# First layer: the weighted head output is read out of PSUM by ScalarE, behind its own square, in place of VectorE

## The chip, the cores and the metric

The kernel runs on one core of one Trainium2 chip. The metric is the device time of one execution in microseconds (us), as the median of several runs of the same program. Five engines work side by side: TensorE (PE in the profile; PEld is its weight load), VectorE (DVE), ScalarE (ACT), GpSimd (POOL) and SyncE (SP), which here only issues DMAs. Each works through its own list of instructions in order and waits on semaphores for the others.

## The reference

A backbone of two layers over 512 latent tokens and 256 context tokens of width 1024. The first layer mixes tokens by differential attention with 8 heads, the second by grouped-query attention. The change is in the first layer, in what follows the attention of one head:

```python
o1 = sweep_attention(qq[..., 0, :], kk[..., 0, :], vv)
o2 = sweep_attention(qq[..., 1, :], kk[..., 1, :], vv)
o = o1 - lam.astype(o1.dtype) * o2
o = rms_norm(o, subln_g) * (1.0 - lam_init)          # over the head's 128 columns
o = o.reshape(o.shape[0], o.shape[1], BRANCH_WIDTH)
return (o * jax.nn.silu(gate)) @ w_out
```

`rms_norm` needs the sum of squares of a head's output and its product with the weight `subln_g`. Everything is computed to float32 accuracy.

## The kernel before, in words

A float32 product is made of three passes on TensorE: each operand is split into a rounded part and a rest (tiles `whi`/`wlo` for weights, `h` for activations, `vhi`/`vlo` for values, `ah`/`al` for attention weights), and hi*hi, hi*lo and lo*hi are added up in PSUM. A split is a ScalarE cast followed by a VectorE subtraction (L225 and L219 for weights, L1062 and L1063 for `ah`/`al`).

The first layer's attention runs from about 75 to 455 us of the span. Per head there are three chunks (`ch`) of two 128-token query blocks: two of latent queries and one of context queries. A chunk is worked off in three stages, which the planner `flow` mixes with projections of later heads:

- **Scores** (`s_units`, L994; L1023 for the context chunk) go into one pair of PSUM tiles, `sc`. VectorE takes the row maximum (L999, L1029), ScalarE the exponential (L1002, L1033), VectorE the reciprocal and the two scalings (L1005, L233, L1009, L1010, L1041), which leave the difference of the two softmaxes in a tile `p`.
- **Transposes** (`tstep`, L1059) put `p` into one of four PSUM banks `bk`; ScalarE and VectorE split it into `ah` and `al` (L1062, L1063).
- **Values** (`mstep`, `pv_mm`, L167): 18 matmuls for a latent chunk (6 for the context chunk) add up the head's output for 256 tokens in a bank. After the last, the bank is read twice and given back:

```python
nc.scalar.activation(ogs[h][:, sl], o, AF.Square)      # L1080: tile sq
scaled(EG0, gT[h][:, sl], o, subg)                     # L1081: tile gT
close(o)
...
def scaled(eng, dst, src, s_):
    if eng == "a":
        nc.scalar.activation(dst, src, AF.Copy, scale=s_)                                          # L231
    else:
        (nc.vector if eng == "v" else nc.gpsimd).tensor_scalar(dst, src, s_, 1.0, ALU.mult, ALU.mult)  # L233
```

`subg` is a column of 128 weights. That is 8 heads x 3 chunks = 24 squares and 24 scalings of 128x256 elements. Later `subln` (`subln_last` for the last head) sums the squares over the head with a matmul of ones (`colsum`: ScalarE cast L404, POOL subtraction L405, TensorE L406 and L407), takes the reciprocal root on ScalarE (L1091, L1093; for the last head L1106, L1108) and multiplies `gT` by it on VectorE (L1094, L1109).

The four banks `bk` are shared by all of it: projections of q, k, v and z (L155), transposes, value sums, sums of squares, the matmuls of the adaptive-norm weights (`grp_mm`, L835, from tile `araw`) and of the layer's gate (`gate0_finish`, L1131 and L1132, then VectorE L1133 and L1134). A bank's next user waits until its last readers are done.

Weights come in by SP's queue into a ring of two buffers, `raw`; a buffer is free for the next load when its cast L225 and its subtraction L219 are done. `gate0_finish` uses the same ring: it loads a bias (`in_ada_b`) into one buffer and a norm weight (`in_post_g`) into the next (L1116).

The order of instructions on each engine is not the program's text order. `flow` writes the steps down by a table of due times, and the scheduler of the Tile layer then orders each engine's instructions by priorities and by its own estimate of when each is ready. So another engine for one instruction can move instructions on all engines.

Of the kernel before, what the change touches and what calls it, by code (L numbers as in the profile page):

```python
# [68 lines left out]
GFIN = (10, 13)  # L69
QLAG = 2.87  # L70
QTR = 5.35
EG0 = 'v'
EP0 = 'v'
EN1 = 'p'
ESW = 'v'
# [12 lines left out]
def tile_backbone(  # L88
# [55 lines left out]
    def close(o):  # L144
        lru.append(held.pop(id(o))[1])
# [83 lines left out]
# [5 lines that stand above are left out]
# [582 lines left out]
    with tc.tile_pool(name="t0", bufs=1) as t0:  # L816
# [233 lines left out]
        def pv_steps(h, at, ch, after, ts, ms):  # L1050
# [15 lines left out]
            def mstep(kt):  # L1066
# [7 lines left out]
                if kt == kts[-2]:  # L1074
# [5 lines left out]
                    nc.scalar.activation(ogs[h][:, sl], o, AF.Square)  # L1080
                    scaled(EG0, gT[h][:, sl], o, subg)  # L1081
                    close(o)
# [733 lines left out]
```

## Time and profile before

| | |
|---|---|
| median of three runs | 792.33 us |
| the profiled execution's own time | 792.09 us |
| its span, first to last instruction | 790.3 us |
| mean granted TensorE clock | 0.998 |
| instructions in the span | 14199 |
| HBM read / written | 70.56 MB / 2.10 MB |

The profile's page gives busy time by engine, the chain of work that ended last, and groups of instructions by line; the trace behind it can be asked for windows of time, for one tile, or for who waited for whom. In a group's row `x24: 459/476/485` is a count and the shortest, median and longest duration in ns; in a row with bars, `| 11.4, 476 | 3.8 <-ACT sq L1080 3.6` is busy time in us, mean duration in ns, then the engine's idle time just before these instructions and what ended it. A row of a timeline begins with the start in us from the span's start and the duration. Matmuls are pipelined: neighbours overlap in such rows, so that a busy share near 100% says that TensorE had something in flight, not that it could not go faster.

### The profile page before, as it was taken

How to read it: one execution, taken by the hardware profiler on the slowest of the kernel's cores; microseconds unless marked ns; L12 is line 12 of the kernel's file. 1: busy time of each engine (PE TensorE's matmuls, PEld its weight loads, DVE VectorE, ACT ScalarE, POOL GpSimd, SP SyncE). 2: the span in 40 equal slices, each digit the busy share in tenths (PEclk: the TensorE clock that was granted, in tenths of full speed). 3: DMA queues.
4: the chain of work that ended last, by engine and by line, in shares of the span. 5: the costliest groups of instructions: out<-in, count | busy, mean ns of one | idle time of the engine just before them, and what ended most of it. 6: DMA issues, size and time to landing. Idle time of an engine off the chain costs nothing.

```text
span 790.3 us, 14199 instructions
## 1 busy us (share of the span) xinstructions
PE 776.0 (98%) x5446; PEld 699.4 (88%) x5446; DVE 544.8 (69%) x988; ACT 455.2 (58%) x994; POOL 286.4 (36%) x386
## 2 busy tenths in 40 slices
PE   8999999999999999999999999999999999999996
PEld 6688888987888898788979998899999999989986
DVE  4656787996888656776588853567458987565634
ACT  5546555665665644765468843565456676676632
POOL 1111443733236331344313311585436554234101
PEclk9999999999999999999999999999999999999999
DMA  9933211141323222233330151041423512010102
GB/s 340 383 101 144 80 54 58 51 134 41 134 80 108 94 81 67 94 107 108 117 97 28 54 209 59 1 141 54 160 82 102 148 46 81 28 54 27 54 27 107
DMA packets 35092, 77.77 MB, mean 98 GB/s; under 512 B 3408, under 2 KB 10064, under 8 KB 35024
## 3 DMA queue, kind: packets, MB, share of 16 engines
q1 hardware_dynamic: 31168, 71.05, 26.8%
q10 hardware_dynamic: 3856, 5.81, 2.1%
q8 instruction: 43, 0.70, 0.4%
q14 instruction: 25, 0.20, 0.1%
HBM read 70.56 MB, written 2.10 MB: 92 GB/s over the span
## 4 chain that ended last, share of the span: by engine, by line
PE 89%; DMA 5%; DVE 2%; ACT 2%; POOL 1%; issue 1%; SPq 0%; DVEq 0%; ACTq 0%; POOLq 0%
PE bk L155 57%; PE bk L167 9%; PE sc L155 8%; PE sc L994 5%; PE bk L1059 3%; PE bk L1558 3%; PE bk L835 1%; DMA xnt<-in_xcT 1%; DMA ag<-in_ada 1%; DMA lamb<-in_a_lam 1%; PE sc L1023 1%; DMA xnt<-in_xlT 1%; POOL wlo L219 1%; DMA raw<-in_b_w 1%; PE bk L407 0%
## 5 line engine op out<-in xcount | busy, mean ns | idle before, releaser
L155 PE MATMUL bk<-whi,h 128*128 128x256 f32 (+1 forms) x1184 | 244.0, 299 | 0.0
L155 PE MATMUL bk<-h,whi 128*128 128x512 f32 (+2 forms) x864 | 228.2, 346 | 0.0
L155 PEld LDWEIGHTS bk<-whi,h 128*128 128x128 f32 x1184 | 191.9, 191 | 10.2 <-issue 3.7
L155 PE MATMUL bk<-wlo,h 128*128 128x256 f32 (+1 forms) x592 | 175.7, 299 | 0.0
L155 PEld LDWEIGHTS bk<-h,whi 128*128 128x128 f32 x864 | 150.5, 189 | 17.0 <-issue 2.7
L155 PE MATMUL bk<-h,wlo 128*128 128x512 f32 (+2 forms) x432 | 149.3, 346 | 0.0
L155 PEld LDWEIGHTS bk<-wlo,h 128*128 128x128 f32 x592 | 112.6, 191 | 4.6 <-issue 1.5
L219 DVE TENSOR_TENSOR wlo<-raw,whi 128x1024 fp32r<-128x1024 f32 (+1 forms) x66 | 82.9, 1258 | 33.5 <-ACT whi L225 33.4
L155 PEld LDWEIGHTS bk<-h,wlo 128*128 128x128 f32 x432 | 81.5, 189 | 7.9 <-issue 1.1
L225 ACT CAST whi<-raw 128x1024 fp32r<-128x1024 f32 x64 | 67.1, 1049 | 32.3 <-PE bk L155 27.9
L999 DVE TENSOR_REDUCE sm<-sc 128x1 f32<-128x768 f32 (+1 forms) x68 | 60.6, 917 | 23.2 <-PE sc L994 23.1
L1002 ACT ACTIVATE p<-sc,sm 128x768 f32<-128x768 f32 (+1 forms) x68 | 59.7, 880 | 23.5 <-DVE sm L999 19.0
L219 POOL TENSOR_TENSOR sz<-sz,za 128x192 f32<-128x192 f32 (+1 forms) x48 | 32.7, 703 | 101.8 <-ACT za L199 101.8
L233 POOL TENSOR_SCALAR p<-p,sm 128x768 f32<-128x768 f32 x32 | 31.6, 987 | 57.3 <-DVE sm L1544 46.0
L1562 DVE TENSOR_TENSOR al<-bk,ah 128x512 fp32r<-128x512 f32 x48 | 32.1, 686 | 18.1 <-ACT ah L1561 17.9
L994 PE MATMUL sc<-qk,qk 64*128 64x384 f32 (+1 forms) x396 | 43.9, 351 | 0.7 <-ACT p L1002 0.7
L219 POOL TENSOR_TENSOR qk<-qr,qk 128x256 fp32r<-128x256 f32 x42 | 32.3, 800 | 33.0 <-ACT qk L889 33.0
L1062 ACT CAST ah<-bk 128x512 fp32r<-128x512 f32 x56 | 31.8, 589 | 20.3 <-PE bk L1059 19.5
L405 POOL TENSOR_TENSOR sqs<-sq,sqs 128x384 fp32r<-128x384 f32 (+2 forms) x16 | 19.4, 1214 | 59.2 <-ACT sqs L404 52.4
L1543 ACT ACTIVATE p<-sc,sm,qrs 128x768 f32<-128x768 f32 x32 | 31.9, 997 | 15.6 <-DVE sm L1540 9.4
L1063 DVE TENSOR_TENSOR al<-bk,ah 128x512 fp32r<-128x512 f32 x56 | 37.2, 681 | 4.4 <-ACT ah L1062 4.2
L219 POOL TENSOR_TENSOR qr<-qr,rope 128x256 f32<-128x256 f32 x28 | 26.0, 948 | 39.0 <-DMA sw<-qr 35.3
(241 smaller groups left out, 1541.1 us busy)
## 6 DMA issues: line engine op xcount, KB each, us to landing
raw<-in_a_w SPq DMA_DIRECT2D x28, 512.0 KB, 3.4
araw<-in_ada_w SPq DMA_DIRECT2D x12, 1024.0 KB, 5.2
raw<-in_b_w SPq DMA_DIRECT2D x20, 512.0 KB, 4.1
ag<-in_ada SPq DMA_DIRECT2D x16, 512.0 KB, 8.0
raw<-in_w_out SPq DMA_DIRECT2D x16, 512.0 KB, 3.5
sw<-qr ACTq DMA_DIRECT2D x32, 128.0 KB, 2.1
gw<-in_ada_w SPq DMA_DIRECT2D x8, 512.0 KB, 4.7
xnt<-in_xlT SPq DMA_DIRECT2D x4, 512.0 KB, 5.6
```

The source lines that it names most:

```text
L155: i = nc.tensor.matmul(o, a, b, start=start, stop=stop)
L167: nc.tensor.matmul(o, v[:, kt + e, c], a[:, e * 256:e * 256 + 256], start=first and i == 0, stop=last and i == 5)
L219: eng.tensor_tensor(dst[:, i:i + n], a[:, i:i + n], b[:, i:i + n], op)
L225: nc.scalar.copy(hi, r)
L233: (nc.vector if eng == "v" else nc.gpsimd).tensor_scalar(dst, src, s_, 1.0, ALU.mult, ALU.mult)
L994: prev = nc.tensor.matmul(sc[m][:, j if nk == T else m, :w], a[r, tok], b[r, c], start=i == 0, stop=i == 2)
L999: nc.vector.tensor_reduce(mx, scv, AX.XY if nk == T else AX.X, ALU.max, negate=True)
L1002: nc.scalar.activation(pv_, scv, AF.Exp, bias=mx, accum_out=l[:, m:m + 1])
L1062: nc.scalar.copy(ah, tr)
L1063: nc.vector.tensor_tensor(al, tr, f32(ah), ALU.subtract)
L1543: nc.scalar.activation(pt.rearrange("p (j n) -> p j n", j=2), scv, AF.Exp, scale=sr, bias=nmx, accum_out=l)
L1562: nc.vector.tensor_tensor(al, tr, f32(ah), ALU.subtract)
```

## The change

One constant is set from VectorE to ScalarE:

```diff
-EG0 = 'v'
+EG0 = 'a'
```

`EG0` is used in one place, L1081 (shown above). So the 24 scalings leave VectorE (`TENSOR_SCALAR`, L233) and become ScalarE `ACTIVATE` instructions with the function `Copy` and the column `subg` as their scale (L231). Nothing else in the text changes, and on each engine the same other instructions remain; but from the first of these scalings on, through the end of the first layer, the scheduler gives all engines another order.

Three places of that order. First ScalarE at the end of head 4 (tile `gT_2808`): rows that stay have no sign, those with + are new there.

```order
 L1080 ACTIVATE sq_3460<-bk_71 128x256
+L231 ACTIVATE gT_2808<-bk_71,subg 128x256
 L404 CAST sqs_3616<-sq_3460 128x384
 L225 CAST whi_3565<-raw_3563 128x1024
 L866 ACTIVATE qr_3329<-bk_70 128x256
 L1080 ACTIVATE sq_3460<-bk_68 128x256
+L231 ACTIVATE gT_2808<-bk_68,subg 128x256
 L1002 ACTIVATE p_3667,sm_3652<-sc_72,sm_3665 128x768
 L1091 ACTIVATE sq_3460<-bk_71,eps 128x384
```

Each scaling stands directly behind the square of the same bank; the exponential L1002 and the root's logarithm L1091 are behind both. The same holds at all 24 places.

Second VectorE in the middle of head 2, where the first half of the layer's gate is made (`gate_0`, `gate_1`; `raw_2159` is the bias, `raw_2161` the norm weight; `raw_2135` and `raw_2141` are the two weight loads ahead of them in the ring).

```order
+L219 TENSOR_TENSOR wlo_2138<-raw_2135,whi_2137 128x1024
 L1029 TENSOR_REDUCE sm_2197<-sc_72 128x2
 L1063 TENSOR_TENSOR al_2156<-bk_68,ah_2155 128x512
-L219 TENSOR_TENSOR wlo_2138<-raw_2135,whi_2137 128x1024
 L931 TENSOR_TENSOR vlo_1945<-bk_71,vhi_1944 128x256
+L1133 TENSOR_TENSOR gate_0_691<-bk_69,raw_2159 128x512
 L219 TENSOR_TENSOR wlo_2144<-raw_2141,whi_2143 128x1024
-L1133 TENSOR_TENSOR gate_0_691<-bk_69,raw_2159 128x512
 L1134 TENSOR_TENSOR gate_0_691<-gate_0_691,raw_2161 128x512
+L1029 TENSOR_REDUCE sm_2205<-sc_73 128x2
 L1063 TENSOR_TENSOR al_2180<-bk_68,ah_2179 128x512
 L1133 TENSOR_TENSOR gate_1_692<-bk_71,raw_2159 128x512
```

The subtraction `wlo_2138`, which frees the buffer for the bias, moves up two places, and the addition of the bias (L1133, `gate_0`) now stands ahead of `wlo_2144`, which frees the buffer for the norm weight. On ScalarE the cast `whi_2137` moves up three places with it; five of the matmuls that read the weights it replaces now stand ahead of the context scores (L1023), not behind them.

Third TensorE a little later, where it needs what VectorE makes there (`bk_68` is read by `al_2180`, `bk_71` by `gate_1`).

```order
+L155 MATMUL bk_70<-h_594,whi_1937 128x512
+L155 MATMUL bk_70<-h_593,wlo_1938 128x512
 L1059 MATMUL bk_68<-ident,p_1915 128x128
 L1059 MATMUL bk_68<-ident,p_2032 128x128
...
-L835 MATMUL bk_70<-araw_1986,s_129 32x512 x4
 L167 MATMUL bk_71<-ah_2155,vhi_1944 128x256 x2
 L167 MATMUL bk_71<-ah_2155,vlo_1945 128x256 x2
...
+L835 MATMUL bk_70<-araw_1986,s_129 32x512 x4
```

The four matmuls L835 stood between the transposes into `bk_68` and the value sum in `bk_71`; now that sum follows the transposes directly, and L835 comes after it.

## The prediction

> **What bounds the kernel now.** I read the page first: busy time by engine, then the chain of work that ended last.
>
> ```profile
> PE 776.0 (98%) x5446; PEld 699.4 (88%) x5446; DVE 544.8 (69%) x988; ACT 455.2 (58%) x994; POOL 286.4 (36%) x386
> PE 89%; DMA 5%; DVE 2%; ACT 2%; POOL 1%; issue 1%; SPq 0%; DVEq 0%; ACTq 0%; POOLq 0%
> ```
>
> TensorE is in flight 98% of the span and holds 89% of the chain; VectorE and ScalarE together hold 4%. An average hides stages, so next come windows over the stretch in which the 24 scalings run (101 to 453 us). The columns are the window, its length, then busy time and count for PE, PEld, DVE, ACT and POOL, the granted clock, the DMA share and GB/s.
>
> ```profile
> 100.00:150.00 50.00, 50.00 (x335) 43.26 (x332) 42.12 (x67) 30.15 (x63) 22.81 (x26) 1.00 0.18 58
> 150.00:200.00 50.00, 48.81 (x364) 42.33 (x363) 41.38 (x70) 30.70 (x69) 20.92 (x25) 1.00 0.27 90
> 200.00:250.00 50.00, 50.00 (x351) 44.14 (x352) 42.03 (x69) 31.40 (x64) 20.59 (x23) 1.00 0.30 102
> 250.00:300.00 50.00, 49.99 (x355) 44.53 (x355) 31.23 (x53) 25.89 (x51) 17.22 (x21) 1.00 0.29 95
> 300.00:350.00 50.00, 48.40 (x352) 42.32 (x351) 38.54 (x72) 32.67 (x73) 17.48 (x22) 1.00 0.27 91
> 350.00:400.00 50.00, 50.00 (x372) 44.84 (x371) 31.56 (x60) 24.74 (x52) 15.27 (x18) 1.00 0.32 106
> 400.00:440.00 40.00, 38.79 (x273) 34.05 (x272) 34.46 (x69) 29.75 (x68) 13.54 (x16) 1.00 0.17 53
> ```
>
> Here VectorE is the fuller of the two (31 to 42 of 50 us), ScalarE has 17 to 25 us free in each 50, and TensorE is idle for only 1.19 + 0.01 + 1.60 + 1.21 = 4.0 us in all. What other engines do reaches the end only through TensorE, so 4.0 us is about the most that relief on VectorE can return. Which waits make up these 4.0 us is in the list of who waited for whom on TensorE (us in total, times, longest):
>
> ```profile
> PE bk L835 <- DVE gT L233: 1.6, 1, 1.6
> PE bk L1059 <- DVE al L1063: 1.1, 1, 1.1
> PE sc L994 <- ACT p L1002: 0.7, 1, 0.7
> PE bk L835 <- DVE al L1063: 0.5, 1, 0.5
> ```
>
> The longest ends with one of the 24 scalings; two end with VectorE's subtraction `al`, one with ScalarE's exponential.
>
> **The change part by part.** VectorE loses 24 instructions, ScalarE gains 24 behind 24 squares that it already does. One row of the tile `gT`, one of the tile `sq` (count, shortest, median and longest ns):
>
> ```profile
> L233 DVE TENSOR_SCALAR gT<-bk,subg x24: 459/476/485, 101.2 to 453.0; 128x256 f32<-128x256 f32 x24
> L1080 ACT ACTIVATE sq<-bk x24: 375/386/423, 100.8 to 452.6; 128x256 f32<-128x256 f32 x24
> ```
>
> *Work.* VectorE gives up 24 x 0.476 = 11.4 us. The new instruction (ScalarE copy, PSUM to SBUF, scaled by a column) is not in the trace. Its neighbours are, by form, within the attention (busy us, mean ns, idle before):
>
> ```profile
> L866 ACT ACTIVATE qr<-bk 128x256 f32<-128x256 f32 x11 | 4.2, 379 | 0.0
> L1033 ACT ACTIVATE p<-sc,sm 128x256 f32<-128x256 f32 x28 | 13.0, 480 | 4.6 <-PE bk L1059 4.6
> L1091 ACT ACTIVATE sq<-bk,eps 128x384 f32<-128x384 f32 x14 | 8.1, 579 | 20.2 <-PE bk L407 20.1
> L197 ACT ACTIVATE za<-za 128x384 f32<-128x384 f32 x14 | 7.4, 527 | 0.3
> ```
>
> The same copy of this size with a constant scale takes 379 ns: the lower bound. An exponential of this size with a column as bias, which also sums, takes 480 ns: the upper bound. A logarithm with a column (579) is 52 ns over one with a constant (527), so I take the square's 386 + 52, near 0.44 us, and 24 x 0.44 = 10.6 us (9.1 to 11.5) on ScalarE. Spread over 350 us this is 1.5 us in each 50, against 17 to 25 free: hidden under TensorE. If that cover were gone, all 10.6 us would show. Likewise VectorE's 11.4 us return nothing by themselves. The sum therefore rests on places where TensorE waits.
>
> [...]
>
> *Place 1, end of head 4: the stall that the change removes.* Timeline of all engines (start, duration):
>
> ```profile
> 321.09 1.81 DVE L999 TENSOR_REDUCE sm<-sc 128x1 f32<-128x768 f32 x2
> 321.28 0.39 ACT L1080 ACTIVATE sq<-bk 128x256 f32<-128x256 f32 x1 [1.12 <-PE bk L167]
> 322.07 0.90 ACT L1002 ACTIVATE p<-sc,sm 128x768 f32<-128x768 f32 x1 [0.41 <-DVE sm L999]
> 322.82 0.47 DVE L233 TENSOR_SCALAR gT<-bk,subg 128x256 f32<-128x256 f32 x1
> 322.96 0.57 ACT L1091 ACTIVATE sq<-bk,eps 128x384 f32<-128x384 f32 x1
> 323.35 1.06 PE L835 MATMUL bk<-araw,s 128*32 128x512 f32 x8 [1.60 <-DVE gT L233]
> 324.34 0.50 PE L155 MATMUL bk<-h,whi 128*128 128x256 f32 x2
> ```
>
> The square is done at 321.67, but VectorE is inside two row maxima until 322.8, so the bank comes free at 323.3 and L835 starts at 323.35. In the changed order the copy follows the square at once: 321.67 + 0.44 = 322.1, L835 at 322.15, that is 1.2 us earlier. What is late next: behind L835 stands a projection (L155) into the bank that the logarithm L1091 reads, and L1091 stays behind the exponential L1002 (0.89 us from start to start). It would end near 322.12 + 0.89 + 0.57 = 323.58, so L155 starts at 323.6 in place of 324.34. Gain 0.7 us, not 1.6.
>
> *Place 2, the gate in head 2: a wait that the new order lengthens.*
>
> ```profile
> 184.21 0.98 PE L1023 MATMUL sc<-qk,qk 64*128 64x256 f32 x12
> 187.06 1.05 ACT L225 CAST whi<-raw 128x1024 fp32r<-128x1024 f32 x1
> 188.15 1.81 DVE L219 TENSOR_TENSOR wlo<-raw,whi 128x1024 fp32r<-128x1024 f32 x1 [0.26 <-ACT whi L225]
> 189.98 0.33 SPq L1116 DMA_DIRECT2D raw<-in_ada_b  x1
> 190.21 1.42 DVE L219 TENSOR_TENSOR wlo<-raw,whi 128x1024 fp32r<-128x1024 f32 x1
> 191.66 0.33 SPq L1116 DMA_DIRECT2D raw<-in_post_g  x1
> 193.12 0.69 DVE L1133 TENSOR_TENSOR gate<-bk,raw 128x512 f32<-128x512 f32 x1 [1.49 <-DMA raw<-in_ada_b]
> 194.77 0.69 DVE L1134 TENSOR_TENSOR gate<-gate,raw 128x512 f32<-128x512 f32 x1 [0.96 <-DMA raw<-in_post_g]
> 195.38 0.68 DVE L1063 TENSOR_TENSOR al<-bk,ah 128x512 fp32r<-128x512 f32 x1
> 195.98 0.68 DVE L1133 TENSOR_TENSOR gate<-bk,raw 128x512 f32<-128x512 f32 x1
> 196.12 0.66 PE L1059 MATMUL bk<-ident,p 128*128 128x128 f32 x4 [1.15 <-DVE al L1063]
> 196.70 1.06 PE L835 MATMUL bk<-araw,s 128*32 128x512 f32 x8
> 197.70 0.51 PE L167 MATMUL bk<-ah,vhi 128*128 128x256 f32 x2
> ```
>
> The page's group of such subtractions has a mean of 1258 ns:
>
> ```profile
> L219 DVE TENSOR_TENSOR wlo<-raw,whi 128x1024 fp32r<-128x1024 f32 (+1 forms) x66 | 82.9, 1258 | 33.5 <-ACT whi L225 33.4
> ```
>
> Each subtraction `wlo` frees a ring buffer; the load after it takes 3.1 us (189.98 to 193.12, 191.66 to 194.77). In this order the two loads overlap. In the changed order the bias's addition stands between the subtractions, so the second load starts only after the first has landed. Part of that is returned: the first cast may start when the moved matmuls are done, near 185.0, not at 187.06. Followed with these durations and 1.26 us for a `wlo`: cast done 186.05, first `wlo` 187.35, bias landed 190.5, addition and second `wlo` done 192.4, norm weight landed 195.5; then L1134 and the maximum L1029 (0.61 each from start to start) and `al`, done 197.4 against 196.06. The value sum L167 waits for the second addition, 198.05 against 197.70, with L835's 1.0 us still to do. Cost 198.05 + 1.0 - 197.70 = 1.4 us (rounded up); 0 at best, if the loads are out of the way earlier; 4.0 if the first `wlo` ends no earlier than before (189.96, and all of the rest 2.6 us later).
>
> *Everything else that is reordered*, on all engines to the end of the layer: I can name no one wait with a size, so 0, with bounds of -2.5 us (the other TensorE waits, 4.0 less Place 1's 1.6) and about +4 us (as much new waiting as there is now). Where TensorE's new order asks for a bank early, the copy helps: after a value sum the bank is free after two ScalarE instructions, 0.39 + 0.44 us, without VectorE's queue between.
>
> *Sum.* 792.09 - 0.7 + 1.4 + 0 = 792.8 us against the profiled execution (span 790.3). The median of the runs, 792.33, lies 0.24 above it, so 793.0.
>
> **Rivals.** *The copy chokes ScalarE* (slower). ScalarE works in order, and behind each copy stand exponentials and `ah` casts that TensorE's next transposes and value sums need. If TensorE had to wait for every one, it would cost 10.6 us, 803.6 with the forecast's other terms; for a third of them 3.5 us: 796.5. It decides where ScalarE has no gap between a copy and what TensorE waits for. For it: one of the four waits above ends with an exponential. Against it: 17 to 25 us free per 50. [...]
>
> *The loads at Place 2 are dearer*: 4.0 in place of 1.4, so 795.6. For it: 1.49 and 0.96 us of VectorE's idle time there already end with these loads. Against it: the moved matmuls free the weight buffer early.
>
> *The waits dissolve* (faster): the bank returns sooner everywhere, VectorE is lighter by 11.4 us and Place 2 costs nothing. Then most of the 4.0 us goes, say 2.8: 789.5. Against it: the new order makes waits of its own.
>
> That the change does something else than it says is no live case: the copy's function is used already (L866) and the new order holds no further table load.
>
> **How the numbers follow.** The forecast has 0.50, the choked ScalarE 0.20, the dearer loads 0.15, the dissolved waits 0.15. The predicted time is the forecast's, 793.0. The range runs from 789.0, below the dissolved waits, to 797.5, past the third of the copies and the dearer loads. Two per cent of 792.33, about what a measurement of this kernel can tell from no change, is 15.8 us; all cases lie within it, even every copy in full. So 0.97 for within 2%; 0.01 for faster, which 4.0 us of idle TensorE hardly allow, and 0.02 for slower.
>
> **What would show it.** Right: 24 L231 rows near 440 ns; L835 at the end of head 4 without a wait of over 1 us; in head 2 a wait of TensorE for `al` or the gate that is longer than 1.15 us; TensorE's idle time from 100 to 440 us at 3 to 6 us. Wrong: TensorE waits behind ScalarE that sum to over 3 us, or a time outside the range.

## The result, and the profile after

The changed kernel takes 796.23 us (median of six runs, 794.71 to 796.55) against 792.66 us for the kernel before, run beside it: a ratio of 1.0042 [1.0027, 1.0057], some 3.5 us slower and inside the two per cent that the prediction gave a chance of 0.97. Two of the six runs of the kernel before took 1075 and 1933 us; the ratio leaves them out. The time lies inside the range, 3.2 us above the forecast. The profiled execution took 796.55 us (span 794.8), 4.46 us over the one before; the lines below are from it.

The new copies, by the tile `gT` (count, shortest, median and longest ns):

```profile
L231 ACT ACTIVATE gT<-bk,subg x24: 466/478/512, 101.1 to 457.4; 128x256 f32<-128x256 f32 x24
```

They take 478 ns, against 476 ns on VectorE. The windows of the layer in which TensorE is idle, to be held against those of before:

```profile
150.00:200.00 50.00, 46.75 (x343) 41.02 (x342) 38.74 (x64) 31.38 (x71) 17.83 (x23) 0.98 0.25 74
200.00:250.00 50.00, 49.43 (x340) 42.80 (x340) 39.38 (x65) 30.19 (x67) 20.80 (x23) 0.98 0.31 102
250.00:300.00 50.00, 49.40 (x367) 44.62 (x366) 31.14 (x50) 27.45 (x56) 19.40 (x23) 1.00 0.31 100
300.00:350.00 50.00, 49.05 (x339) 42.67 (x338) 37.04 (x69) 33.24 (x75) 14.65 (x19) 1.00 0.30 96
400.00:440.00 40.00, 38.69 (x278) 34.17 (x277) 32.57 (x69) 30.59 (x72) 10.48 (x12) 1.00 0.19 62
```

VectorE (third figure) is a little emptier, ScalarE a little fuller, as the change says. TensorE (first figure) is idle for 3.25 + 0.57 + 0.60 + 0.95 + 1.31 = 6.7 us from 100 to 440 us, where it was 4.0. And a column has changed that was 1.00 before: the granted clock is 0.98 in two windows. Who waited for whom on TensorE:

```profile
PE bk L1059 <- DVE al L1063: 3.0, 2, 2.7
PE sc L1350 <- POOL xn L1342: 0.7, 1, 0.7
PE bk L835 <- ACT gT L231: 0.7, 1, 0.7
PE bk L167 <- DVE al L1063: 0.6, 2, 0.3
PE bk L1059 <- DVE p L1041: 0.6, 1, 0.6
PE bk L167 <- ACT sz L964: 0.6, 1, 0.6
PE bk L155 <- ACT sq L1091: 0.3, 1, 0.3
```

The wait at the end of head 4 (L835) has gone from 1.6 to 0.7 us, with 0.3 us for the logarithm L1091 behind it; the one at the gate (L1059) from 1.1 to 2.7 us. Waits of 0.6 us for `p` and for `sz` and three of about 0.3 us for `al` are new. One wait of the full list is left out here, that for `sqx` (L618): 2.0 us in total against 0.9. It lies in the first 10 us, ahead of every row that changed, and is made up at once, since the next wait ends at 13.8 us in both kernels.

The gate, from the timelines of VectorE, SyncE and TensorE (start, duration):

```profile
186.68 1.23 DVE L219 TENSOR_TENSOR wlo<-raw,whi 128x1024 fp32r<-128x1024 f32 x1 [1.69 <-ACT whi L225]
187.93 0.33 SPq L1116 DMA_DIRECT2D raw<-in_ada_b  x1
191.26 0.69 DVE L1133 TENSOR_TENSOR gate<-bk,raw 128x512 f32<-128x512 f32 x1 [1.61 <-DMA raw<-in_ada_b]
191.86 1.22 DVE L219 TENSOR_TENSOR wlo<-raw,whi 128x1024 fp32r<-128x1024 f32 x1
193.11 0.33 SPq L1116 DMA_DIRECT2D raw<-in_post_g  x1
196.50 0.69 DVE L1134 TENSOR_TENSOR gate<-gate,raw 128x512 f32<-128x512 f32 x1 [3.42 <-DMA raw<-in_post_g]
197.71 0.68 DVE L1063 TENSOR_TENSOR al<-bk,ah 128x512 fp32r<-128x512 f32 x1
198.45 1.10 PE L1059 MATMUL bk<-ident,p 128*128 128x128 f32 x4 [2.68 <-DVE al L1063]
199.20 0.78 PE L167 MATMUL bk<-ah,vhi 128*128 128x256 f32 x2
201.91 0.40 PE L167 MATMUL bk<-ah,vhi 128*128 128x256 f32 x2
```

The chain is the one forecast: bias, its addition, second subtraction, second load, multiplication, `al`. VectorE stands still for 3.42 us with the second load in flight. The last two rows show something that was not forecast: the same pair of matmuls spans 0.78 us at 199.20 and 0.40 us at 201.91. Windows of 2 us tell why (granted clock third from the right):

```profile
198.00:200.00 2.00, 1.55 (x8) 1.55 (x9) 2.00 (x5) 1.40 (x5) 0.00 (x0) 0.62 0.01 4
200.00:202.00 2.00, 2.00 (x11) 2.00 (x11) 1.75 (x7) 0.59 (x1) 0.00 (x0) 0.52 0.89 270
202.00:204.00 2.00, 2.00 (x19) 1.61 (x18) 0.90 (x3) 0.00 (x0) 0.00 (x0) 1.00 0.86 277
```

After the wait TensorE gets half its clock: it is 0.50 in each of the two single microseconds from 199 to 201 us, and 0.62 and 0.52 over 2 us each come to about 3.4 us at one half. The halved windows hold 8 and 11 matmuls where the whole one holds 19 (the first has 0.45 us of the wait in it, and the matmuls are of different kinds; the pair above compares like with like). At half speed 3.4 us do the work of 1.7, and take 0.002 off the mean clock of the run. Two of the six runs have a mean clock of 0.998 and 0.999 and take 794.93 and 794.71 us; the other four have 0.996 or 0.997 and take 796.18 to 796.55. So the halving is worth about 1.5 us, and happens in most runs, not all. That the first two are without it is inferred from their mean clock; windows exist for the profiled run alone.

### The profile page after: what moved, and what is told of

Read it like the earlier page. It is cut to its first block, busy times and chain, and to the rows that moved or that the text cites. A ratio compares the mean times of both kernels' runs of the same rounds, so it can differ in the third digit from the quotient of the medians.

```text
span 794.8 us, 14182 instructions
## 1 busy us (share of the span) xinstructions
PE 776.4 (98%) x5446; PEld 699.9 (88%) x5446; DVE 536.6 (68%) x964; ACT 460.0 (58%) x1018; POOL 281.3 (35%) x386
## 4 chain that ended last, share of the span: by engine, by line
PE 87%; DVE 5%; ACT 3%; DMA 2%; POOL 1%; issue 1%; SPq 0%; DVEq 0%; ACTq 0%; POOLq 0%
PE bk L155 55%; PE sc L155 10%; PE bk L167 8%; PE sc L994 5%; PE bk L1558 3%; PE bk L1059 3%; PE bk L835 1%; DMA xnt<-in_xlT 1%; DVE al L1063 1%; POOL wlo L219 1%; DVE wlo L219 1%; DMA raw<-in_b_w 1%; ACT p L1002 1%; PE sc L1023 1%; PE bk L406 1%
## 5 line engine op out<-in xcount | busy, mean ns | idle before, releaser
L219 DVE TENSOR_TENSOR wlo<-raw,whi 128x1024 fp32r<-128x1024 f32 (+1 forms) x66 | 81.2, 1233 | 39.4 <-ACT whi L225 38.9
L1002 ACT ACTIVATE p<-sc,sm 128x768 f32<-128x768 f32 (+1 forms) x68 | 59.8, 884 | 29.3 <-DVE sm L999 25.9
L233 POOL TENSOR_SCALAR p<-p,sm 128x768 f32<-128x768 f32 x32 | 31.6, 988 | 57.2 <-DVE sm L1544 45.9
L994 PEld LDWEIGHTS sc<-qk,qk 64*128 64x128 f32 x396 | 32.8, 185 | 8.0 <-issue 2.9
```

What stands on the lines that cost most here:

```text
L219: eng.tensor_tensor(dst[:, i:i + n], a[:, i:i + n], b[:, i:i + n], op)
L994: prev = nc.tensor.matmul(sc[m][:, j if nk == T else m, :w], a[r, tok], b[r, c], start=i == 0, stop=i == 2)
L1002: nc.scalar.activation(pv_, scv, AF.Exp, bias=mx, accum_out=l[:, m:m + 1])
```

## The experiments

The first four were timed on one chip against the kernel before at 792.43 us, the last four on one chip against 792.99 us.

**Scaling on ScalarE in heads 0 and 1 alone.** Only 6 of the 24 copies move, those ahead of the gate.

```diff
-scaled(EG0, gT[h][:, sl], o, subg)
+scaled('a' if h < 2 else 'v', gT[h][:, sl], o, subg)
```

> Only heads 0 and 1 (6 of the 24 scalings) go to ScalarE; every engine's order is the changed kernel's as far as the gate in head 2 and beyond the transposes that wait there, and the old kernel's from late in head 3 on. Theory A (the loss is the gate's second load, issued one landing later because the bias's addition stands between the two weight subtractions, and the slower TensorE clock right after that wait): nearly all of the loss with a quarter of the copies, 795 to 796.5 us, with the TensorE wait for the subtraction al near 2.7 us. Theory B (the copies' own time on ScalarE delays what TensorE waits for): 6/24 of 3.6 us, 793.5 us.

Measured: 797.59 us, ratio 1.0060 [1.0048, 1.0073], 1.1 us past theory A's range and 4 us past theory B. A quarter of the copies brings more than the whole loss. From its waits on TensorE and its windows:

```profile
PE bk L1059 <- DVE al L1063: 2.4, 1, 2.4
PE bk L835 <- DVE gT L233: 1.6, 1, 1.6
```

```profile
198.00:200.00 2.00, 1.89 (x12) 1.68 (x13) 2.00 (x6) 1.46 (x5) 0.00 (x0) 0.82 0.17 39
200.00:202.00 2.00, 2.00 (x10) 1.80 (x9) 1.96 (x7) 0.17 (x1) 0.00 (x0) 0.50 1.05 301
```

The long wait at the gate and the halved clock are there; so is the old 1.6 us at the end of head 4, since that copy is on VectorE again. The loss does not grow with the number of copies. Its one run at a mean clock of 0.998 took 796.19 us, the four at 0.996 and 0.997 took 797.32 to 797.67.

**Scaling on ScalarE in heads 2 to 7 alone.** The same edit with `h >= 2`; 18 copies move, and the rows at the gate keep their old order.

> Heads 2 to 7 (18 of the 24 scalings) go to ScalarE, heads 0 and 1 stay on VectorE; at the gate in head 2 every engine has the old order. Theory A: no long wait there, no slower clock, 792 to 793.5 us. Theory B: 18/24 of 3.6 us, 795.3 us.

Measured: 791.54 us, ratio 0.9988 [0.9980, 0.9997]. That is a little under theory A's range and far from theory B. The wait at the gate is close to that of before (1.3 us against 1.1), and Place 1 keeps its gain:

```profile
PE bk L1059 <- DVE al L1063: 1.3, 1, 1.3
PE bk L835 <- ACT gT L231: 0.7, 1, 0.7
```

**All 24 copies on ScalarE, the bias addition held behind the second subtraction.** The changed kernel, with one more rule for the scheduler; `lw` is the last weight subtraction issued before.

```diff
-                nc.vector.tensor_tensor(gate0[v][:, sl], o, b, ALU.add)
+                with tc.issue_after(lw):
+                    nc.vector.tensor_tensor(gate0[v][:, sl], o, b, ALU.add)
```

> All 24 scalings on ScalarE as in the changed kernel; the one thing added is that VectorE's addition of the gate's bias may only be issued behind the last weight subtraction ahead of it in the ring of load buffers. The order is the changed kernel's up to that place and again from late in head 3. Theory A: the two loads overlap again, the TensorE wait there falls from 2.7 to about 1.3 us or less, no slower clock, 792.5 to 794 us. Theory B: unchanged, 796 us.

Measured: 791.48 us, ratio 0.9986 [0.9977, 0.9995]: better than either theory said, and by the two ratios (1.0042 less 0.9986) some 4.4 us below the changed kernel with the same 24 copies. Its copies take the same median, 478 ns. First its waits, then the windows of the gate:

```profile
PE bk L835 <- ACT gT L231: 0.7, 1, 0.7
PE bk L1059 <- DVE p L1041: 0.6, 1, 0.6
PE bk L167 <- DVE gate L1133: 0.5, 1, 0.5
```

```profile
150.00:200.00 50.00, 48.94 (x365) 42.32 (x364) 40.89 (x70) 32.53 (x73) 18.71 (x22) 1.00 0.28 90
200.00:250.00 50.00, 50.00 (x354) 44.20 (x353) 41.05 (x65) 31.52 (x69) 19.95 (x25) 1.00 0.31 106
```

The clock is whole, the gate's wait is 0.5 us, and the wait for `p` (context softmax of head 1) is still there. VectorE and SyncE at the gate:

```profile
189.82 1.80 DVE L219 TENSOR_TENSOR wlo<-raw,whi 128x1024 fp32r<-128x1024 f32 x1 [0.24 <-ACT whi L225]
191.54 0.68 DVE L1133 TENSOR_TENSOR gate<-bk,raw 128x512 f32<-128x512 f32 x1
191.65 0.33 SPq L1116 DMA_DIRECT2D raw<-in_post_g  x1
194.75 0.69 DVE L1134 TENSOR_TENSOR gate<-gate,raw 128x512 f32<-128x512 f32 x1 [2.54 <-DMA raw<-in_post_g]
```

The two loads do not overlap again, as theory A had it: the second goes out at 191.65 us, when the bias is already there (its addition starts at 191.54 without a wait). What is gained is that the second subtraction ran while the bias was on its way, and not behind its addition, so that the second load starts 1.5 us earlier than in the changed kernel (193.11). This kernel and the changed one differ on TensorE only in rows 1235 to 1795 of its 5324. With the copies the same, the loss lies in the order around the gate and what follows from it.

**One copy alone**, the one at the end of head 4, with the condition `(h, ch) == (4, 2)`.

> One scaling alone goes to ScalarE, that of head 4's context chunk, where the old kernel had its longest TensorE wait (1.6 us, for VectorE's scaling); orders differ from the old kernel's only for some 50 us behind it. Theory A with the prediction's Place 1: that wait falls to about 0.5 us and the next limit, the bank read by the logarithm, gives part of it back: 0.7 us faster, 791.9 us. Theory B: 0.15 us slower or the same, 792.7 us.

Measured: 791.48 us, ratio 0.9989 [0.9981, 0.9998]. The timeline at that place:

```profile
321.19 0.38 ACT L1080 ACTIVATE sq<-bk 128x256 f32<-128x256 f32 x1 [1.12 <-PE bk L167]
321.47 0.47 ACT L231 ACTIVATE gT<-bk,subg 128x256 f32<-128x256 f32 x1
321.99 1.07 PE L835 MATMUL bk<-araw,s 128*32 128x512 f32 x8 [0.34 <-ACT gT L231]
322.86 0.57 ACT L1091 ACTIVATE sq<-bk,eps 128x384 f32<-128x384 f32 x1
323.49 0.50 PE L155 MATMUL bk<-h,whi 128*128 128x256 f32 x2 [0.43 <-ACT sq L1091]
```

Against the kernel before the square starts 0.09 us earlier (321.28), L835 1.36 us (323.35), the projection behind it 0.85 us (324.34): about half a microsecond is taken back by the logarithm L1091, as forecast. The time is 0.95 us below the kernel before, 0.4 below theory A. One copy gives as much as 18 or 24 where the gate's order is kept: the others bring nothing on balance.

**The order alone, with no copy on ScalarE.** The kernel before, with the second subtraction put off until the first bias addition is issued and the next `al` behind the multiplication by the norm weight.

```diff
-        pieces(eng, lo, r, f32(hi), ALU.subtract)
+        calls.append(hi); later.append(lambda: pieces(eng, lo, r, f32(hi), ALU.subtract)) if len(calls) == 13 else pieces(eng, lo, r, f32(hi), ALU.subtract)
...
-                nc.vector.tensor_tensor(al, tr, f32(ah), ALU.subtract)
+                with tc.issue_after(hold.pop()) if hold else nullcontext(): nc.vector.tensor_tensor(al, tr, f32(ah), ALU.subtract)
...
                 nc.vector.tensor_tensor(gate0[v][:, sl], o, b, ALU.add)
-                nc.vector.tensor_tensor(gate0[v][:, sl], gate0[v][:, sl], g, ALU.mult)
+                with tc.issue_after(last_of(nc.vector)) if later else nullcontext(): [later.pop()() for _ in later[:]]
+                nc.vector.tensor_tensor(gate0[v][:, sl], gate0[v][:, sl], g, ALU.mult); (half, v) == (0, 0) and hold.append(last_of(nc.vector))
```

> The kernel before, with all 24 copies still on VectorE, but with VectorE's rows at the gate put in the order of the changed kernel: the bias addition, then the second weight subtraction, then the norm weight's multiplication, then `al`. TensorE's rows differ from the kernel before only between rows 1211 and 1842. Theory A (the change loses by this order alone, through the second load that waits for the second subtraction, and by the halved clock that follows the long wait): TensorE waits 2.4 to 2.9 us for `al` near 195 us, and the time is 793.7 to 794.3 us where the clock stays whole and 795.2 to 796.2 us where it halves for 3.4 us. Theory B (the copies on ScalarE have a part in the loss): 792.4 us or up to 793 us, and no halved clock.

Measured: 799.49 us, ratio 1.0083 [1.0069, 1.0097]: slower by 6.5 us, past what either theory said. Theory B's time and its whole clock are out, and no copy moved. Theory A has the sign and both parts, and missed the size. Timelines of VectorE, SyncE and TensorE, then two windows (in this kernel's text the bias addition stands on L1132):

```profile
188.00 1.81 DVE L219 TENSOR_TENSOR wlo<-raw,whi 128x1024 fp32r<-128x1024 f32 x1 [0.26 <-ACT whi L225]
193.29 0.69 DVE L1132 TENSOR_TENSOR gate<-bk,raw 128x512 f32<-128x512 f32 x1 [3.15 <-DMA raw<-in_ada_b]
195.14 0.33 SPq L1116 DMA_DIRECT2D raw<-in_post_g  x1
195.74 0.33 SPq L223 DMA_DIRECT2D raw<-in_a_w  x1
199.63 0.69 DVE L1134 TENSOR_TENSOR gate<-gate,raw 128x512 f32<-128x512 f32 x1 [3.32 <-DMA raw<-in_post_g]
200.98 0.66 PE L1059 MATMUL bk<-ident,p 128*128 128x128 f32 x4 [3.76 <-DVE al L1063]
```

```profile
200.00:202.00 2.00, 1.02 (x9) 1.02 (x10) 2.00 (x5) 0.32 (x1) 1.91 (x2) 1.00 1.04 408
202.00:204.00 2.00, 2.00 (x14) 1.79 (x14) 2.00 (x8) 0.27 (x1) 0.12 (x1) 0.54 0.86 296
```

Here the first subtraction is not moved up; it ends at 189.8 us, not at 187.9 as in the changed kernel, so the bias lands 2.0 us later; and the second load, with a weight's load issued 0.6 us behind it, needs 4.5 us (195.14 to 199.63), where it needed 3.4. TensorE waits 3.8 us, the clock halves, and TensorE idles 2.3 us more from 200 to 250 us (47.68 us busy, 50.00 before). It is a harder form of the same order, so it shows that the order alone can cost all of the loss, not how much of it.

**Two buffers of their own for the gate's loads**: in the kernel before, in the changed kernel, and with the copies of heads 2 to 7 alone.

```diff
-            r = wp.tile([P, 1024], F32, tag="raw", name=nm("raw"), bufs=2)
-            nc.sync.dma_start(r[:, :512], src.partition_broadcast(P))
-            return r[:, :512]
+            r = t0.tile([P, 512], F32, tag="grow", name=nm("grow"), bufs=2)
+            nc.sync.dma_start(r, src.partition_broadcast(P))
+            return r
```

> The kernel before, with the gate's four loads in two buffers of their own, so that none waits for a weight to be split. Copies stay on VectorE. Theory A (the wait of 1.3 to 1.5 us that the kernel before has at the gate comes from the shared buffers): that wait is gone, Place 1 keeps its 1.8 us, and the time is 791.0 to 791.6 us. Theory B (a wait taken away there comes back a little later at the next limit): 792.2 to 792.6 us.

> The changed kernel, all 24 copies on ScalarE, with the gate's four loads in two buffers of their own. Theory A (the shared buffers carry the whole loss): no wait over 0.8 us and no halved clock near 195 us, the gain of Place 1 kept, 790.2 to 791.4 us. Theory B (the copies on ScalarE cost something of their own): 794 us or more.

> The kernel before with the copies of heads 2 to 7 alone on ScalarE and the gate's loads in two buffers of their own: the version that should be the best of both. Theory A (each wait taken away is worth what it was): 790.0 to 791.0 us, lowest of all. Theory B (the gains fall together, the next limit takes them back): 791.3 to 791.8 us, no better than either alone.

Measured: 802.32 us (1.0124 [1.0110, 1.0138]), 799.77 us (1.0088 [1.0074, 1.0101]) and 799.45 us (1.0082 [1.0068, 1.0096]). No theory held: only the second kernel's theory B has the time within its words (794 us or more), and not for its reason. The loads, free earlier, made the scheduler write another order from TensorE's row 405 on, long before the gate. The windows of the changed kernel with these buffers:

```profile
100.00:150.00 50.00, 45.59 (x302) 38.41 (x301) 34.43 (x52) 24.60 (x53) 18.75 (x23) 1.00 0.16 47
150.00:200.00 50.00, 47.27 (x351) 41.87 (x349) 37.72 (x65) 31.54 (x70) 14.78 (x20) 0.97 0.25 80
200.00:250.00 50.00, 50.00 (x340) 43.05 (x339) 40.36 (x69) 33.96 (x77) 20.94 (x26) 1.00 0.32 107
```

From 100 to 165 us TensorE now idles for over 7 us; the gate, near 200 us here, has no wait at all (50.00 busy). In the other two TensorE has no wait at the gate either, but one behind it, of 1.3 us at 211 us and of 0.7 us at 210 us. So these three show that the gate's wait does go with the shared buffers, and that this is no better version; as a test of what the copies cost they are confounded. Between the first two, which share those early waits, the kernel with the copies on ScalarE is 2.6 us ahead; their orders differ as well, ahead of the gate and behind it, so that this is no price of the copies. Their halved clocks fit the earlier ones: of the third kernel's runs, those at a mean clock of 0.998 took 798.70 and 798.93 us, those at 0.996 took 799.96 and 799.97.

## Why the prediction was right in range and wrong in its sum

*Work, hidden.* Right. The copy is 0.478 us, not 0.44, at the upper bound (0.480); that makes 11.5 us on ScalarE in place of 10.6. All of it is hidden: 1, 18 and 24 copies give 791.48, 791.54 and 791.48 us where the gate's order is kept. The choked ScalarE is refuted, although the time came out where it had put it (796.5): six copies lose more than 24. The multiplication by a column is here as fast on ScalarE as on VectorE (478 against 476 ns).

*Place 1.* Right in mechanism, and near in size. Gain 0.7 us forecast, with the next limit L1091; the one copy alone measured 0.95 us, and TensorE then waits 0.43 us for L1091. In the changed kernel its waits there fell by the same 0.7 us (1.6 to 0.7 and 0.3).

*Place 2.* The chain was right in each step. Forecast: norm weight landed 195.5, `al` done 197.4; measured 196.50 and 198.39, both about 1 us later. The first subtraction ended 0.56 us later than forecast (187.91), which fits the 0.6 us by which the wait for `p` had already pushed TensorE back, and each of the two loads took 0.2 to 0.3 us longer. The wait grew from 1.15 to 2.68 us, by 1.5, for a term of 1.4. What the prediction did not have is that behind this wait the clock is halved (0.62 and 0.52 in the two windows of 2 us): about 1.5 us more in most runs, by their mean clocks. So the place costs 3, not 1.4: the wait was priced right and the clock behind it was left out.

*Everything else 0.* This is the step that failed in the sum, beside the clock. TensorE's idle time from 100 to 440 us went up by 2.7 us, to 6.7, outside the 3 to 6 that the prediction gave as its sign. The gate's 1.5 less Place 1's 0.7 explain 0.8 of it; 1.9 us are small waits that the new order made: 0.6 for `p` in head 1, 0.6 for `sz` (238 us) and three of about 0.3 for `al` (253, 257 and 413 us), less 0.2 by which a wait for `p` near 410 us got shorter. With the gate held, the wait for `sz` and the first two for `al` are gone from the list, the third and that for `p` stay: so more than half of them goes with the gate's order. I had no name for them, and took 0 in a range of -2.5 to +4; the run was near +2. That the time still lies in the range is luck in part: its upper end was drawn to hold two rivals, 796.5 and 795.6, neither of which came about.

*Sum of the profiled execution*: 2.7 us of idle time, 1.5 to 1.7 us of halved clock, and a few tenths in the second layer (TensorE's wait for `xn`, L1342, 0.7 in place of 0.4) come to 4.5 to 4.7, for a measured 4.46 us.

*Rivals.* The time is near that of the dearer loads (795.6), but by chance. Their condition was a first subtraction that ends no earlier than before (189.96); it ended at 187.91, and the loads took 3.3 and 3.4 us against 3.1. The order alone is the run that meets it (189.81), and there the wait grew by 2.6 us, to 3.76. The dissolved waits came only in the versions that keep the gate's order, and gave 0.9 to 1.0 us below the kernel before, not 2.8.

*What stays open.* The price of the halved clock comes from comparing runs of the same kernel that have it with those that don't, and the runs without it are told by their mean clock alone. No kernel was run that keeps the long wait and always avoids the halving. How the loss divides between it and the waits is so far worked out, not tested apart.

## What to carry to other kernels

A move of work between engines is priced in two parts, the work itself and the order that the scheduler writes because of it; here the first was free and the second was the loss, nearly all of it from one place that the order showed beforehand and whose price was more than the wait itself. Look for an in-order engine that comes to stand between two loads that share buffers: what it waits for then also holds back the next load. When such a move pays at one place, move that one instruction, or pin the order where it turns (here 791.48 us both ways), and look at the whole order again after any repair, since freeing the buffers made over 7 us of waiting elsewhere.

## What the runs showed of the hardware

Here the length of a wait had a price beyond itself. Waits of TensorE of 1.15 to 1.6 us (the kernel before) left the clock at 1.00. After 2.4 to 2.7 us (heads 0 and 1, the changed kernel) and 3.8 us (the order alone) it fell to 0.5 for about 3.4 us (over 2 us each 0.82, 0.50 and 0.83; 0.62 and 0.52; 0.54 and 0.61). By the runs' mean clocks it did so in most runs but not in each (four of six of the changed kernel, four of five of heads 0 and 1), at 1.2 to 1.5 us a time. No trace has a lone wait between 1.6 and 2.4 us, so what a wait of that length does is open. In the changed kernel with buffers of its own it also fell after two shorter waits close together:

```profile
156.00:158.00 2.00, 1.03 (x7) 0.71 (x6) 1.09 (x3) 2.00 (x7) 2.00 (x4) 1.00 0.69 242
158.00:160.00 2.00, 0.41 (x4) 0.17 (x2) 1.97 (x4) 2.00 (x7) 2.00 (x3) 1.00 0.00 0
160.00:162.00 2.00, 1.83 (x8) 1.83 (x9) 1.93 (x5) 1.62 (x4) 1.48 (x3) 0.51 0.00 0
```

TensorE is idle for 0.97 us of the first window and 1.59 us of the second, with some work between. In the kernel before with these buffers the same pair of waits was followed by about 7 us at one half (0.93 over 150 to 200 us). In the order alone the halving began a microsecond after the wait was over: TensorE is back at 200.98 us, and the clock is 1.00 until 202.
